# Sums of weight blocks in two seven-product SwiGLUs: VectorE additions replaced by accumulating transfers

## The chip, the cores and the metric

One core of one Trainium2 chip runs the whole program in one launch. The metric is the device time of that launch in microseconds (us). PE is TensorE's matmul side, PEld its weight loading, DVE is VectorE, ACT is ScalarE, POOL is GpSimd, SP is SyncE, whose queue issues all the transfers of the kernel before.

## The reference

The program computes two layers of a hybrid backbone over 512 latent tokens and 256 context tokens of width 1024, in float32. Each layer is a half-step SwiGLU, a token-mixing block (Fourier mixing, latent attention, windowed attention) and a second half-step SwiGLU. What matters here is the SwiGLU:

```
def swiglu(x, w1, w3, w2):
    return (jax.nn.silu(x @ w1) * (x @ w3)) @ w2

def macaron_half(h, m, i, g, w1, w3, w2):
    y = swiglu(modulate(rms_norm(h, g), m[:, 3 * i], m[:, 3 * i + 1]), w1, w3, w2)
    return h + 0.5 * m[:, 3 * i + 2, None, :] * y
```

The hidden width is 2816, that is 22 blocks of 128 columns of w1 and w3. The last SwiGLU of the program needs the 512 latent tokens alone; the first SwiGLU of the second layer works on all 768 tokens.

## The kernel before, in words

All activations are kept transposed, 128 features by tokens. Each float32 operand of a matmul is split into a high and a low part (float32r), and three matmuls (high by high, high by low, low by high) stand for one exact product: `mm3`, lines 396 to 398. A weight block of 128x1024 is loaded by SP into a buffer called `raw` (five buffers, `raws=5`, line 314) and split into a buffer called `w` (four buffers, `wslots=4`): the high part by an ACT cast (line 403, or line 406 with a scale), the low part by a DVE subtraction (line 404, or 407). After the subtraction the raw buffer is free; after the last matmul that reads it, the w buffer is free.

Two of the four SwiGLUs, both in the second layer, are written with seven block products in place of eight (`ffn7`, line 806): the first over all 768 tokens (halves of 384 columns), the second over the 512 latent tokens (halves of 256 columns). In them the 22 blocks of hidden columns are taken as 11 pairs. The first pair is plain (`first_pair`). Each of the other ten (`pair`, line 950) has four weight blocks a11, a12, a21 and a22 of 128x1024, and seven products, each of 24 matmuls, in this order of the program: B11 with a11, B21 with a12, E with minus (a21 + a22 + a11), t3 with (a11 + a21), t1 with (a21 + a22), t4 with a22, B22 with (a21 + a22 + a11 + a12). The products go to two PSUM tiles X and Y. Several of them add on top of what is there after ScalarE has copied the old content out (`snapshot`, line 876): E and t1 add to Y, t4 adds to X, so t4 has to wait for the copy of X that is made after t3. `gated` adds, applies silu and multiplies (lines 883 to 885); `parts` splits the result (lines 857, 858).

Between B11 and B21 in program order stands `middle()`: the down projection of the pair before, with two more weight blocks of w2 through the same raw and w buffers (`unit`, line 384) and 8 outputs per stream, each of six matmuls into one of four PSUM banks B and one DVE evacuation (line 895). So a pair takes weights in this order: a11, two blocks of w2, a12, then what E, t3, t1, t4 and B22 need.

The order of instructions on each engine is set by a scheduler that goes by priority (program order) and by its own estimate of when operands are ready; on the chip each engine runs its queue strictly in that order. Which buffer of `raw` or `w` a tile gets is whichever comes free, in that same order.

In the kernel before, the sums are made by four DVE additions per pair (lines 967, 968, 969 and 971) in a fifth raw tile `s1` and, in place, in the loaded blocks.

Of the kernel before, what the change touches and what calls it, by code (L numbers as in the profile page):

```python
# [12 lines left out]
ALU = mybir.AluOpType  # L13
# [299 lines left out]
class Builder:  # L313
# [480 lines left out]
    def block(self, src):  # L794

        r = self.mp.tile([128, 1024], F32, tag="raw", name=self.name("raw"), bufs=self.raws)
        if src is not None:
            self.nc.sync.dma_start(r, src)
        return r

    def split_block(self, r, scale=None):
# [4 lines left out]
    def ffn7(self, l, i, n, t, gate, nxt, streams=(X_COLS, C_COLS), split=None, late=None):  # L806
# [10 lines left out]
        nc = self.nc  # L817
        mp13, w2 = self.a["w13s"][i], self.a["w2"][l, i]
# [26 lines left out]
        def operand(name, k):  # L845
            tile_, cols = {"B11": (n[k], n1), "B21": (n[k + 4], n1), "B22": (n[k + 4], n2),
                           "t1": (tt.get((k, "u")), n1), "t3": (tt.get((k, "u")), n2),
                           "t4": (tt.get((k, "v")), n1), "E": (tt.get((k, "v")), n2)}[name]
            return [p[:, cols] for p in tile_]


        def gtiles(j):
            for f in (2 * j, 2 * j + 1):
                g[f] = self.hl(T, "g")

        def parts(f, s, cols):
            nc.scalar.copy(g[f][0][:, cols], s[:, cols])  # L857
            nc.vector.tensor_sub(g[f][1][:, cols], s[:, cols], g[f][0][:, cols].bitcast(F32))

        def product(bank, w, name, start):  # L860

            for x in range(2):
                for k in range(4):
                    self.mm3(bank[:, x * 512:x * 512 + wd], [w[:, p, x * 512 + k * 128:x * 512 + k * 128 + 128] for p in range(2)],
                             operand(name, k), start and k == 0, k == 3, not start)
# [7 lines left out]
        def snapshot(bank, base):  # L873
            y = self.m3(2 * wd, base=base)
            v = y.rearrange("p (x c) -> p x c", x=2)
            nc.scalar.copy(v, both(bank))
            return y, v

        def gated(s, cols, bank, y, sign):

            z = self.m3(2 * wd, base="z")
            zv = z.rearrange("p (x c) -> p x c", x=2)
            nc.vector.tensor_tensor(out=zv, in0=both(bank), in1=y[1], op=ALU.add)
            self.last_silu = nc.scalar.activation(s[:, cols], zv[:, 0], AF.Silu, scale=sign)
            nc.vector.scalar_tensor_tensor(out=s[:, cols], in0=zv[:, 1], scalar=sign, in1=s[:, cols], op0=ALU.mult, op1=ALU.mult)
            self.free(z)
# [59 lines left out]
        def done_with(j, name):  # L946
            if j == np_ - 1:
                self.free([tt.pop((k, name)) for k in range(4)])

        def pair(j, middle):  # L950
            fs = (2 * j, 2 * j + 1)
            src = mp13[j]
            add = nc.vector.tensor_add
            Y, X = (self.ps("S", (j + x) % 2) for x in range(2))
            r11 = self.block(src[0, 0])
            product(Y, self.split_block(r11), "B11", True)
            middle()
            y0 = snapshot(Y, "y")
            gtiles(j)
            s = [self.m3(base="silu") for _ in range(2)]  # L960
            r12 = self.block(src[0, 1])
            product(X, self.split_block(r12), "B21", True)
            r21, r22, s1 = self.block(src[1, 0]), self.block(src[1, 1]), self.block(None)
            gated(s[0], n1, X, y0, 1.0)
            self.free(y0[0])
            parts(fs[0], s[0], n1)
            add(s1, r21, r22)
            add(r21, r11, r21)
            add(r11, s1, r11)
            product(Y, self.split_block(r11, -1.0), "E", False)  # L970
            add(r12, r11, r12)
            y1 = snapshot(Y, "y")
            product(X, self.split_block(r21), "t3", True)
            w0 = snapshot(X, "y")
            product(Y, self.split_block(s1), "t1", False)
            done_with(j, "u")
            gated(s[1], n2, Y, w0, -1.0)
            self.free(w0[0])
            product(X, self.split_block(r22), "t4", False)
            done_with(j, "v")  # L980
            gated(s[1], n1, X, y1, -1.0)
            self.free(y1[0])
            parts(fs[1], s[1], slice(halves[0][0], halves[1][1]))
            product(Y, self.split_block(r12), "B22", False)
            self.last_silu = nc.scalar.activation(s[0][:, n2], Y[:, 0:wd], AF.Silu)
            nc.vector.tensor_mul(s[0][:, n2], s[0][:, n2], Y[:, 512:512 + wd])
            parts(fs[0], s[0], n2)
            self.free(s)
# [6 lines left out]
        def middle(j):  # L995
            def go():
                ws, fs = second(j), (2 * j, 2 * j + 1)
                for d in range(8):
                    for cols in streams:
                        down(fs, ws, d, cols)  # L1000
                self.free([g.pop(f) for f in fs])
            return go

        for j in range(1, np_ - 1):
            pair(j, middle(j - 1))

        fs = (NF - 2, NF - 1)
        if x_only:
            pair(np_ - 1, middle(np_ - 2))
        else:  # L1010
            held = {}

            def go():
                held["ws"], held["fs"] = second(np_ - 2), (NF - 4, NF - 3)
                for d in range(8):
                    down(held["fs"], held["ws"], d, X_COLS)

            pair(np_ - 1, go)
            for d in range(8):
                down(held["fs"], held["ws"], d, C_COLS)  # L1020
            self.free([g.pop(f) for f in held["fs"]])
# [878 lines left out]
```

## Time and profile before

| | us |
|---|---|
| median of 3 runs | 2759.79 |
| lowest and highest run | 2757.23 to 2761.97 |
| the profiled execution, its own time | 2759.59 |
| its span, first to last instruction | 2757.9 |

In the profiled execution TensorE's matmuls are busy for 2681.3 us (97% of the span), VectorE 1937.3 us (70%), ScalarE 1015.0 us (37%) and GpSimd 280.6 us (10%). The mean granted TensorE clock was 0.988. All transfers but the instruction fetches are issued by SP. A busy share is an average over stages with different limits; a stage is read from the stretch in which it runs. The pairs of the first seven-product SwiGLU lie between about 1610 and 2060 us, those of the second between about 2433 and 2730 us.

### The profile page before, as it was taken

Reading aid. Unit: us, or ns where it says so; the run is one execution under the profiler, and the core shown is the slowest. Engines: PE = TensorE matmul, PEld = TensorE weight load, DVE = VectorE, ACT = ScalarE, POOL = GpSimd, SP = SyncE. Lnnn points to the kernel's source line nnn. Section 1 sums busy time; section 2 is a strip of 40 time slices with the busy share of each in tenths; the row PEclk is TensorE's granted clock in tenths of the full one; section 3 lists DMA queues with packets and bytes.
Section 4 is the critical chain, followed back from the end, with each engine's and each line's share of the span. In section 5 each row is a group of like instructions: output and inputs, shape, how many; then the busy total and the mean of one; then the engine's idle time right before and its main releaser. Section 6 shows DMA issues by size and latency. Waiting matters only on the chain.

```text
span 2757.9 us, 40164 instructions
## 1 busy us (share of the span) xinstructions
PE 2681.3 (97%) x16028; PEld 2346.5 (85%) x16028; DVE 1937.3 (70%) x3385; ACT 1015.0 (37%) x1773; POOL 280.6 (10%) x372
## 2 busy tenths in 40 slices
PE   7999999999989999999999999999999989999999
PEld 5788888888867788888888889999998777889998
DVE  8986776655685658988663687676756675598886
ACT  4411211124665642111121443333335665554443
POOL 5100000011352210000000100000001352100000
PEclk9899999999989999999999999999999999999999
DMA  7432433211200025545321111212122210123322
GB/s 247 163 131 99 152 124 102 90 54 60 73 24 23 13 88 181 168 136 198 125 92 62 54 54 62 76 61 72 62 76 67 70 32 24 39 71 114 99 93 91
DMA packets 78671, 249.60 MB, mean 91 GB/s; under 512 B 8978, under 2 KB 10642, under 8 KB 78484
## 3 DMA queue, kind: packets, MB, share of 16 engines
q1 hardware_dynamic: 78484, 247.03, 27.1%
q8 instruction: 126, 2.06, 0.3%
q14 instruction: 61, 0.50, 0.1%
HBM read 244.90 MB, written 2.10 MB: 90 GB/s over the span
## 4 chain that ended last, share of the span: by engine, by line
PE 88%; DVE 6%; ACT 2%; issue 2%; DMA 1%; POOL 1%; SPq 0%; DVEq 0%; ACTq 0%; POOLq 0%
PE S L398 16%; PE S L396 16%; PE S L397 16%; PE B L396 11%; PE B L398 11%; PE B L397 11%; PE B L1409 3%; PE B L1560 2%; DVE w L404 1%; PE B L1528 1%; DVE junk L483 1%; ACT P L1397 0%; PE B L1453 0%; ACT w L403 0%; DMA ada<-in_w_ada 0%
## 5 line engine op out<-in xcount | busy, mean ns | idle before, releaser
L403 ACT CAST w<-raw 128x1024 fp32r<-128x1024 f32 x349 | 359.6, 1043 | 961.6 <-issue 539.0
L397 PE MATMUL S<-nlo,w 128*128 128x256 f32 (+2 forms) x1968 | 653.9, 333 | 7.0 <-DVE nlo L605 4.0
L398 PE MATMUL S<-nhi,w 128*128 128x256 f32 (+2 forms) x1968 | 652.5, 332 | 1.8 <-DVE w L404 1.7
L396 PE MATMUL S<-nhi,w 128*128 128x256 f32 (+2 forms) x1968 | 644.3, 333 | 9.1 <-DVE silu L915 3.9
L404 DVE TENSOR_TENSOR w<-raw,w 128x1024 fp32r<-128x1024 f32 x349 | 424.0, 1227 | 119.3 <-ACT w L403 117.1
L398 PE MATMUL B<-ghi,w 128*128 128x512 f32 (+1 forms) x1232 | 425.1, 346 | 0.8 <-DVE w L404 0.8
L397 PE MATMUL B<-glo,w 128*128 128x512 f32 (+1 forms) x1232 | 425.8, 346 | 0.0
L396 PE MATMUL B<-ghi,w 128*128 128x512 f32 (+1 forms) x1232 | 419.9, 348 | 2.7 <-ACT ghi L857 2.0
L397 PEld LDWEIGHTS S<-nlo,w 128*128 128x128 f32 x1968 | 371.9, 189 | 44.3 <-DVE nlo L605 7.5
L396 PEld LDWEIGHTS S<-nhi,w 128*128 128x128 f32 x1968 | 369.1, 189 | 45.0 <-DVE silu L915 4.5
L398 PEld LDWEIGHTS S<-nhi,w 128*128 128x128 f32 x1968 | 372.0, 189 | 38.8 <-DVE w L404 6.4
L691 DVE SCALAR_TENSOR_TENSOR h<-B,g,h 128x512 f32<-128x512 f32 (+1 forms) x352 | 208.2, 615 | 179.2 <-PE B L398 178.7
L396 PEld LDWEIGHTS B<-ghi,w 128*128 128x128 f32 x1232 | 230.6, 188 | 33.5 <-ACT ghi L857 2.4
L398 PEld LDWEIGHTS B<-ghi,w 128*128 128x128 f32 x1232 | 231.9, 188 | 31.2 <-DVE w L404 1.0
L397 PEld LDWEIGHTS B<-glo,w 128*128 128x128 f32 x1232 | 232.0, 188 | 30.2 <-issue 1.0
L895 DVE SCALAR_TENSOR_TENSOR h<-B,g,h 128x512 f32<-128x512 f32 (+1 forms) x264 | 170.1, 658 | 121.4 <-PE B L398 121.1
L483 DVE CUSTOM_DVE_ANT_0 junk<-ada,bc,mpart 128x768 f32<-128x768 f32 x238 | 245.6, 1032 | 6.3 <-DMA ada<-in_w_ada 1.3
L532 POOL TENSOR_TENSOR sq<-sq,sq 128x512 f32<-128x512 f32 (+1 forms) x38 | 42.8, 1126 | 1134.8 <-ACT sq L528 1133.7
L483 DVE CUSTOM_DVE_ANT_0 junk<-ada,bc,sml 128x256 f32<-128x256 f32 x238 | 118.7, 499 | 19.9 <-DMA ada<-in_w_ada 15.0
L1392 DVE TENSOR_REDUCE nm<-S 128x1 f32<-128x768 f32 (+3 forms) x120 | 94.5, 793 | 42.0 <-PE S L398 33.0
L1403 POOL TENSOR_SCALAR P<-P,rd 128x768 f32<-128x768 f32 (+3 forms) x120 | 96.7, 808 | 240.0 <-DVE rd L1402 185.1
L1397 ACT ACTIVATE P<-S,nm 128x768 f32<-128x768 f32 (+3 forms) x120 | 93.0, 776 | 56.0 <-DVE nm L1392 31.6
(273 smaller groups left out, 4450.2 us busy)
## 6 DMA issues: line engine op xcount, KB each, us to landing
raw<-in_w SPq DMA_DIRECT2D x176, 512.0 KB, 3.6
ada<-in_w_ada SPq DMA_DIRECT2D x171, 384.0 KB, 4.3
raw<-in_w13s SPq DMA_DIRECT2D x88, 512.0 KB, 3.7
raw<-in_w_out SPq DMA_DIRECT2D x16, 512.0 KB, 4.1
ada<-in_ada SPq DMA_DIRECT2D x16, 384.0 KB, 6.6
raw<-in_w_in_t SPq DMA_DIRECT2D x10, 512.0 KB, 3.5
raw<-in_dftx SPq DMA_DIRECT2D x8, 512.0 KB, 3.5
ada<-in_ada SPq DMA_DIRECT2D x8, 256.0 KB, 5.6
```

What stands on the lines that cost most here:

```text
L396: mm(out, lhs[0], rhs[0], start=start, stop=False, skip_group_check=more)
L397: mm(out, lhs[0], rhs[1], start=False, stop=False, skip_group_check=more)
L398: mm(out, lhs[1], rhs[0], start=False, stop=stop, skip_group_check=more)
L403: nc.scalar.copy(hi, src)
L404: nc.vector.tensor_sub(lo, src, hi.bitcast(F32))
L483: nc.vector.tensor_tensor_reduce(out=self.junk[:, 0:w.shape[1]], in0=w, in1=v, scale=1.0, scalar=init, op0=ALU.mult, op1=ALU.add, accum_ou ...
L691: nc.vector.scalar_tensor_tensor(out=self.h[d][:, c0:c1], in0=ps[:, 0:c1 - c0], scalar=gate()[:, d, s:s + 1], in1=self.h[d][:, c0:c1], op0 ...
L895: nc.vector.scalar_tensor_tensor(out=self.h[d][:, c0:c1], in0=ps[:, 0:c1 - c0], scalar=gate()[:, d, s:s + 1], in1=self.h[d][:, c0:c1], op0 ...
L1392: self.last_max = nc.vector.tensor_reduce(out=nm, in_=ps[:, c0:c1], axis=AX.X, op=ALU.max, negate=True)
L1397: self.last_exp = nc.scalar.activation(P, ps[:, c0:c1], AF.Exp, bias=nm, scale=1.0, accum_out=den)
L1403: nc.gpsimd.tensor_scalar(out=P, in0=P, scalar1=rd, scalar2=1.0, op0=ALU.mult, op1=ALU.mult)
L1409: mm(outs[y], lhs[y], rhs[y], start=start, stop=stop)
```

## The change

The four DVE additions go. A new helper, `block_sum`, loads the first block of a sum with a plain transfer from SP and then adds each further block with a transfer issued from GpSimd's queue that accumulates into the same raw buffer. Blocks that are in several sums are loaded again for each. Everything else (splits, products, copies, gating) stays.

```
     def block(self, src):
         r = self.mp.tile([128, 1024], F32, tag="raw", ...)
-        if src is not None:
-            self.nc.sync.dma_start(r, src)
+        self.nc.sync.dma_start(r, src)
+        return r
+
+    def block_sum(self, *srcs):
+        r = self.block(srcs[0])
+        for src in srcs[1:]:
+            self.nc.gpsimd.dma_start(out=r, in_=src, accum_op=ALU.add)
         return r
...
-            src = mp13[j]
-            add = nc.vector.tensor_add
+            (a11, a12), (a21, a22) = ([mp13[j, m, q] for q in range(2)] for m in range(2))
...
-            r11 = self.block(src[0, 0])
-            product(Y, self.split_block(r11), "B11", True)
+            product(Y, self.split_block(self.block(a11)), "B11", True)
...
-            r12 = self.block(src[0, 1])
-            product(X, self.split_block(r12), "B21", True)
-            r21, r22, s1 = self.block(src[1, 0]), self.block(src[1, 1]), self.block(None)
+            product(X, self.split_block(self.block(a12)), "B21", True)
...
-            add(s1, r21, r22)
-            add(r21, r11, r21)
-            add(r11, s1, r11)
-            product(Y, self.split_block(r11, -1.0), "E", False)
-            add(r12, r11, r12)
+            product(Y, self.split_block(self.block_sum(a21, a22, a11), -1.0), "E", False)
             y1 = snapshot(Y, "y")
-            product(X, self.split_block(r21), "t3", True)
+            product(X, self.split_block(self.block_sum(a11, a21)), "t3", True)
             w0 = snapshot(X, "y")
-            product(Y, self.split_block(s1), "t1", False)
+            product(Y, self.split_block(self.block_sum(a21, a22)), "t1", False)
...
-            product(X, self.split_block(r22), "t4", False)
+            product(X, self.split_block(self.block(a22)), "t4", False)
...
-            product(Y, self.split_block(r12), "B22", False)
+            product(Y, self.split_block(self.block_sum(a21, a22, a11, a12)), "B22", False)
```

## Rows read from the trace of the kernel before

**Rows 1.** The profile's page: the span, and TensorE's part of its first section.

```profile
span 2757.9 us, 40164 instructions
...
PE 2681.3 (97%) x16028; PEld 2346.5 (85%) x16028; DVE 1937.3 (70%) x3385; ACT 1015.0 (37%) x1773; POOL 280.6 (10%) x372
```

**Rows 2.** Busy time by stretch: stretch, length, engines, granted clock, DMA share, GB/s.

```profile
1610.00:2060.00 450.00, 448.60 (x2546) 427.26 (x2545) 304.61 (x385) 144.96 (x185) 0.00 (x0) 1.00 0.21 68
2464.00:2712.00 248.00, 247.66 (x1712) 228.27 (x1711) 200.55 (x245) 104.74 (x151) 0.00 (x0) 1.00 0.32 103
2433.00:2464.00 31.00, 29.73 (x206) 27.12 (x205) 28.42 (x36) 13.87 (x20) 0.00 (x0) 1.00 0.31 102
```

**Rows 3.** DVE groups by line, 2464 to 2712 us: count, busy, mean ns, idle before.

```profile
L404 DVE TENSOR_TENSOR w<-raw,w 128x1024 fp32r<-128x1024 f32 x63 | 75.5, 1220 | 10.5 <-ACT w L403 10.5
...
L971 DVE TENSOR_TENSOR raw<-raw,raw 128x1024 f32<-128x1024 f32 x8 | 9.8, 1226 | 0.3
L967 DVE TENSOR_TENSOR raw<-raw,raw 128x1024 f32<-128x1024 f32 x8 | 9.8, 1226 | 2.4 <-DMA raw<-in_w13s 1.7 <-DVE silu L885 0.6
L968 DVE TENSOR_TENSOR raw<-raw,raw 128x1024 f32<-128x1024 f32 x8 | 9.7, 1219 | 0.0
L969 DVE TENSOR_TENSOR raw<-raw,raw 128x1024 f32<-128x1024 f32 x8 | 9.7, 1216 | 0.0
```

**Rows 4.** Line 798, the loads of the blocks a11 to a22, whole span.

```profile
L798 SPq DMA_DIRECT2D raw<-in_w13s x88: 327/328/328, 1499.6 to 2706.4; - x88
...
DMA to landing us min/median/max: 3.3/3.7/5.5
```

**Rows 5.** SP's queue in order of time, 2430 to 2560 us: one pair to the next.

```profile
2500.98 11.13 SPq L388 DMA_DIRECT2D raw<-in_w  x2
2512.92 18.12 SPq L798 DMA_DIRECT2D raw<-in_w13s  x4
2532.51 11.15 SPq L388 DMA_DIRECT2D raw<-in_w  x2
```

**Rows 6.** ScalarE in order of time, one pair of the second SwiGLU.

```profile
2540.73 2.00 ACT L403 CAST w<-raw 128x1024 fp32r<-128x1024 f32 x2 [7.47 <-PE B L398]
2542.63 0.58 ACT L876 COPY y<-S 128x512 f32<-128x512 f32 x1
2543.11 1.05 ACT L403 CAST w<-raw 128x1024 fp32r<-128x1024 f32 x1
2544.50 0.59 ACT L876 COPY y<-S 128x512 f32<-128x512 f32 x1 [0.34 <-PE S L398]
...
2553.33 1.04 ACT L403 CAST w<-raw 128x1024 fp32r<-128x1024 f32 x1
...
2559.15 1.06 ACT L406 ACTIVATE w<-raw 128x1024 fp32r<-128x1024 f32 x1 [2.67 <-DVE raw L969]
```

**Rows 7.** VectorE in order of time, the same pairs.

```profile
2529.47 1.21 DVE L407 SCALAR_TENSOR_TENSOR w<-raw,w 128x1024 fp32r<-128x1024 f32 x1
2530.61 0.74 DVE L895 SCALAR_TENSOR_TENSOR h<-B,g,h 128x512 f32<-128x512 f32 x1
...
2542.09 3.49 DVE L404 TENSOR_TENSOR w<-raw,w 128x1024 fp32r<-128x1024 f32 x3
...
2555.77 1.22 DVE L404 TENSOR_TENSOR w<-raw,w 128x1024 fp32r<-128x1024 f32 x1
```

**Rows 8.** TensorE in order of time: first down matmul, first of t4, first of B22.

```profile
2528.38 0.39 PE L397 MATMUL B<-glo,w 128*128 128x512 f32 x1
...
2547.14 0.28 PE L396 MATMUL S<-cvhi,w 128*128 128x256 f32 x1
...
2550.00 0.28 PE L396 MATMUL S<-nhi,w 128*128 128x256 f32 x1
```

**Rows 9.** Busy time by stretch: the program's first loads, all engines of DMA at work.

```profile
14.00:18.00 4.00, 2.93 (x14) 2.84 (x15) 3.58 (x8) 3.17 (x5) 0.00 (x0) 1.00 1.02 400
```

**Rows 10.** GpSimd's groups by line, whole span: its longest and its shortest instructions.

```profile
L475 POOL TENSOR_TENSOR mprod<-ada,bc 128x768 f32<-128x768 f32 x14 | 30.7, 2203 | 32.0 <-DMA ada<-in_ada 20.2 <-issue 8.5 <-DVE a L236 2.6
...
L1403 POOL TENSOR_SCALAR P<-P,rd 128x256 f32<-128x256 f32 x24 | 11.4, 478 | 23.5 <-DVE rd L1402 14.8 <-PE B L1495 2.5 <-ACT es L1400 1.8
```

**Rows 11.** ScalarE in order of time, one pair of the first SwiGLU.

```profile
1703.97 1.04 ACT L403 CAST w<-raw 128x1024 fp32r<-128x1024 f32 x1
...
1733.33 2.00 ACT L403 CAST w<-raw 128x1024 fp32r<-128x1024 f32 x2
```

## The prediction

> **What bounds the kernel now.** I read the page's first section first: matmuls are busy for 97% of the span [rows 1], so only a stage in which TensorE waits can gain much. Then the stretches of the two edited SwiGLUs [rows 2]. In the first, TensorE is busy 448.6 of 450 us; in the second 247.7 of 248 us over about eight pairs, after a first pair with 29.7 of 31. The granted clock is 1.00 throughout, its upper level of 2.4 GHz. VectorE is busy for two thirds to four fifths there, and GpSimd runs nothing. The reader should see that VectorE is not the bound of these pairs: its four additions [rows 3] have almost no idle time ahead of them and none of it reaches TensorE. What could be won in these stretches is TensorE's whole idle time, 1.4 + 0.3 + 1.3 = 3.0 us.
>
> Next I read how far ahead of TensorE the weights are. The queue of SP [rows 5] shows a pair of the second SwiGLU every 31.5 us (2500.98 to 2532.51). Six loads per pair, 512 KB each, keep the DMA engines busy for 0.32 of the time [rows 2]. A load lands 3.7 us after its issue, 3.3 at best and 5.5 at worst [rows 4]. The kernel is bound by TensorE with weights that are ready early, and the question is whether they still are.
>
> **Removed.** Four additions of 1.22 us [rows 3] in each of 20 pairs: 20 x 4 x 1.22 = 98 us of VectorE time. TensorE's work hides it, so it is worth at most the 3.0 us above; I take 1.5.
>
> **Added.** Per pair the loads of a11 to a22 go from 4 plain ones to 7 plain ones from SP and 7 accumulating ones from GpSimd; with the two blocks of w2 that is 16 transfers in place of 6. Three more issues on SP, 0.33 us each [rows 4], delay nothing, because that queue spends its time waiting for buffers. Five raw buffers now serve 9 tiles per pair; before it was 7. GpSimd's queue is empty in these stretches [rows 2], so nothing else waits behind the new instructions. But an accumulation cannot start before the one ahead of it in the same buffer has landed. So GpSimd's queue waits, and the sums behind the waiting one (t3 and t1 behind E, then B22) wait with it. B22 is a chain of one load and three accumulations.
>
> **Price of one accumulation, x.** The trace has no transfer from GpSimd and none that adds, so I bound it. It moves the same bytes as a load, which takes 3.7 us [rows 4]; I see no reason for less. Above that come two unknowns. It may also have to read the destination: 0 to one more pass of the engines, where a pass is 0.32 x 248 / 48 loads = 1.65 us [rows 2]. And GpSimd has to prepare it: from nothing to its longest instruction, 2.2 us; its short ones take 0.48 us [rows 10]. So x lies between 3.7 and 3.7 + 1.65 + 2.2 = 7.5 us. I take a full second pass and a preparation near the short instructions: 3.7 + 1.65 + 0.65 = 6.0 us.
>
> The Trainium skill, page "DMA: Bandwidth & Descriptors", section "Anatomy of one DMA — SWDGE (gpsimd) path", gives 2.0 us plus the bytes over 436 GB/s for one transfer from GpSimd, which is an estimate of 3.2 us for these blocks, without the addition. By it the chain of B22 would be hidden and the time unchanged; no run here shows it yet, and the sum does not use it.
>
> **Does it fit?** In the second SwiGLU, B22's raw buffer is the one that a12 gives back. (Five tiles earlier: a12, E, t3, t1, t4, B22.) a12 is cast at 2553.33 [rows 6], and its subtraction ends at 2555.77 + 1.22 = 2557.0 [rows 7]. The cast of B22 stands at 2543.11 in the pair before [rows 6], so at 2574.6 in this one. Between them lie 17.6 us; a load and three accumulations need 3.7 + 3x. Up to x = 4.6 us nothing waits. Beyond it ScalarE stands at B22's cast, and behind that cast in its queue is the copy of X (2544.50), which t4 needs at 2547.14 [rows 6, 8]. The copy is done 0.6 us after its start, so the cast may begin 2.4 us late: up to x = 5.4 us this is hidden as well. Beyond that, t4 and everything after it on TensorE is late. The late end also delays a12's split of the next pair, so it is a loop: each pair takes 31.5 + 3 (x - 5.4) us.
>
> A second wait runs into the same one. E's buffer comes from the B22 before it, free at 2542.09 + 3.49 = 2545.6 [rows 7]; its load and two accumulations are ready at 2549.3 + 2x, and its cast is at 2559.15 [rows 6], so x = 4.9 us is where VectorE begins to stand at E's subtraction. Behind that is the first evacuation of the down projection, 1.1 us later [rows 7]. Four banks cover it for a few us, and a pair that is stretched by the first loop gives this one the same time back, so I add nothing for it.
>
> In the first SwiGLU the same loop has more room: from a12's split (cast at 1703.97, done some 3 us later) to B22's cast (the second of two from 1733.33, so 1734.3) are 27.4 us [rows 11], which fit up to x = 7.9 us. I count nothing there.
>
> **Sum.** 3 x (6.0 - 5.4) = 1.8 us per pair, ten pairs: +18. Less 1.5 for the additions: 2759.59 + 16.5 = 2776 us against the profiled execution, whose time stands 0.2 us from the median of the runs.
>
> **Rivals.**
>
> *Hidden after all (not slower).* If x is at most 5.4 us, nothing reaches TensorE, and the 3.0 us of idle time bound the gain: 2757 to 2762 us. For it: an unloaded transfer lands in 3.3 us, and the preparation may overlap the wait. The same comes out at x = 6.0 if the scheduler puts B22's cast behind the copy of X. Then only the product's own start counts, 2550.00 + 31.5 [rows 8] less 2.3 us for cast and subtraction, which fits up to x = 6.2 us. Against it: 16 transfers per pair share the engines, and B22's first accumulation queues behind those of t3 and t1.
>
> *The DMA engines become the bound.* If an accumulation reads source and destination one after the other, it costs two passes. By the share of the rows nine plain transfers take 9 x 1.65 = 14.9 us and seven doubled ones 23.1 us: 38.0 us in a pair of 31.5 us, 6.5 us x 10 pairs = +65, 2825 us. Against it: with many loads at once the engines moved 400 GB/s [rows 9], 1.31 us per block, by which it is 9 x 1.31 + 7 x 2.62 = 30.1 us and still fits, barely. It decides from some 2.4 to 2.8 us of engine time per accumulation. The Trainium skill, "Collectives: The Full Stack", section "The bandwidth ceiling", says that a reducing transfer needs two source reads on the same ring and so runs at half the rate of a copy; that speaks for this rival, and no row of this trace bears on it.
>
> *A slow accumulation.* At the upper end, x = 7.5 us, the loop gives 3 x 2.1 x 10 = +63, 2822 us, with the first SwiGLU still just clear of it.
>
> *Faster.* More than 0.2% would need 5.5 us, and both stretches hold 3.0 us of idle time; only another order of instructions elsewhere could give the rest.
>
> **How the numbers follow.** About 0.2% (5.5 us) is what a measurement of this kernel can tell from no change. Chances: an accumulation of 5.5 to 6.8 us, slower by up to 42 us, 0.41; hidden, 0.38; engines bound or x above 6.8 us, 0.18; faster 0.03. Of the first case a little (0.01) lies under 5.5 us. So faster 0.03, same 0.39, slower 0.58. I predict the likeliest case, 2776 us, its own range 2762 to 2801. The range over the cases goes from 2756 (the hidden case with nearly the whole 3.0 us gained) to 2825 (the engines bound by the rows' share, and the upper bound of x).
>
> **What would show it.** Right: DVE lines 967 to 971 gone; GpSimd with 140 transfers; in the second SwiGLU pairs of about 33 us, ScalarE idle ahead of B22's cast with an accumulating transfer as releaser, TensorE idle ahead of t4; the first SwiGLU with pairs as before. Hidden: pairs of 31.5 us and accumulations that land in 5 us. Engines bound: a DMA share near 1 in the second SwiGLU, plain loads that land in much more than 3.7 us, waits spread over all weights. Wrong altogether: waits in the first SwiGLU too, so x above 7.9 us, or an order in GpSimd's queue that holds one sum behind another.

## The result, and the profile after

The changed kernel takes 2840.31 us (median of 4 runs, 2829.44 to 2846.82) against 2759.67 us before: a ratio of 1.0284, 95% interval 1.0264 to 1.0305. The forecast was 2776 us in 2756 to 2825; the direction and the place were right, the size was not, and the time lies 15 us beyond the range.

First the profile's page of the changed kernel: the span and engine totals, beside [rows 1], then GpSimd's DMA queue (packets, MB, the share of 16 engines' span), and two issue rows with the median us from issue to landing.

```profile
span 2836.2 us, 40637 instructions
...
PE 2707.3 (95%) x16028; PEld 2365.6 (83%) x16028; DVE 1852.5 (65%) x3305; ACT 1016.6 (36%) x1773; POOL 403.6 (14%) x512
...
q0 software_dynamic: 20160, 73.41, 14.9%
...
raw<-in_w13s SPq DMA_DIRECT2D x148, 512.0 KB, 4.9
raw<-in_w13s POOLq DMA_DIRECT2D x140, 512.0 KB, 6.7
```

VectorE's busy time is 85 us lower, and that bought nothing: the span is 78 us longer, while TensorE's busy time grew by 26 us.

Busy time by stretch, in the columns of [rows 2]: the first seven-product SwiGLU, then the second.

```profile
1610.00:2060.00 450.00, 449.28 (x2553) 428.45 (x2554) 264.50 (x343) 143.43 (x185) 58.75 (x67) 1.00 0.76 180
2482.00:2770.00 288.00, 248.18 (x1564) 224.73 (x1563) 150.16 (x198) 96.97 (x137) 43.90 (x51) 0.92 0.85 210
```

The first is as before: TensorE busy for all but 0.7 us. The second was busy for 247.7 of 248 us; now 40 of 288 us are idle, and the granted clock is 0.92. SP's queue gives the pair there, beside [rows 5]:

```profile
2482.25 6.02 SPq L388 DMA_DIRECT2D raw<-in_w  x2
...
2761.72 6.50 SPq L388 DMA_DIRECT2D raw<-in_w  x2
```

From the first of these rows to the second are seven pairs: 279.47 / 7 = 39.9 us each, in place of 31.5. Ten pairs 8.4 us longer would be 84 us, close to the loss of 80.6 us.

What sets the 39.9 us is in the chain of work that ended last (start, us, what):

```profile
2547.53 1.05 ACT w L403
2548.60 1.24 DVE w L404
2549.85 8.00 DMA raw<-in_w13s
2557.92 0.60 issue
2558.52 5.47 DMA raw<-in_w13s
2563.99 0.39 issue
2564.38 5.49 DMA raw<-in_w13s
2569.88 0.39 issue
2570.27 7.36 DMA raw<-in_w13s
2577.87 0.78 issue
2578.66 0.59 ACT y L882
2579.29 0.39 PE S L396
...
2587.90 9.05 DMA raw<-in_w13s
```

Read it as a ring: a12 is cast and subtracted, its buffer takes B22's load, three accumulations follow one at a time, then come the copy of X, t4 and B22 (2579.29 to 2585.27), and the next a12 is cast and subtracted. This turn of the ring takes 38.05 us (2549.85 to 2587.90), and its chain 27.8 us (2549.85 to 2577.63), of which the load alone takes 8.00. Each accumulation follows the transfer before it after 0.4 to 0.7 us, so GpSimd's queue did not hold this chain back. The turn before took longer, 46.0 us (2503.89 to 2549.85), with a chain of 33.7 us:

```profile
2503.89 8.60 DMA raw<-in_w13s
...
2528.66 8.89 DMA raw<-in_w13s
```

Six of B22's chains lie on the chain of work that ended last; their loads took 8.0 to 9.05 us. In three of the pairs after 2617 us it runs through E's sum and its cast instead, as here:

```profile
2636.61 1.06 ACT w L406
```

ScalarE's queue at the end of B22's chain, beside [rows 6]:

```profile
2577.70 1.04 ACT L403 CAST w<-raw 128x1024 fp32r<-128x1024 f32 x1 [5.93 <-DMA raw<-in_w13s]
2578.66 0.58 ACT L882 COPY y<-S 128x512 f32<-128x512 f32 x1
```

ScalarE stood 5.93 us at B22's cast, and the copy of X follows right behind it, as the prediction had them. TensorE's waits in 2482 to 2770 us (who waited for what: total us, times, longest) show that most of its idle time is not ahead of t4 (line 882) but ahead of E's product, for E's cast and subtraction (lines 406, 407):

```profile
PE S L396 <- ACT w L406: 25.0, 7, 4.9
PE S L396 <- ACT y L882: 10.2, 5, 5.0
PE S L398 <- DVE w L407: 4.4, 7, 0.8
```

How long a load or an accumulation takes depends on what runs beside it. GpSimd's queue in one early pair of the first SwiGLU:

```profile
1666.38 0.88 POOL L804 DMA_DIRECT2D raw<-in_w13s  x1 [10.12 <-DVE h L901]
1672.15 0.87 POOL L804 DMA_DIRECT2D raw<-in_w13s  x1 [4.89 <-DMA raw<-in_w13s]
```

There, with no other transfer issued beside them, one accumulation follows another after 5.77 us. In the second SwiGLU one lands 5.2 us after its issue at best, 7.1 in the median, 9.7 at worst, and a plain load of the same blocks takes 5.2 us in the median where it took 3.7 [rows 4]. These medians mix several chains. B22's load is among the slowest of the plain ones: it is issued while the sums of E, t3 and t1 are under way, and in its 8 us the DMA share (second number from the end) is 1.04, all the engines at work:

```profile
2549.85:2557.85 8.00, 8.00 (x47) 6.96 (x46) 0.92 (x2) 0.59 (x1) 1.77 (x2) 1.00 1.04 254
```

### The profile page after: what moved, and what is told of

Its sections match the earlier page's. It is cut to its first block, busy times and chain, and to the rows that moved or that the text cites. A ratio compares the mean times of both kernels' runs of the same rounds, so it can differ in the third digit from the quotient of the medians.

```text
span 2836.2 us, 40637 instructions
## 1 busy us (share of the span) xinstructions
PE 2707.3 (95%) x16028; PEld 2365.6 (83%) x16028; DVE 1852.5 (65%) x3305; ACT 1016.6 (36%) x1773; POOL 403.6 (14%) x512
## 3 DMA queue, kind: packets, MB, share of 16 engines
q0 software_dynamic: 20160, 73.41, 14.9%
## 4 chain that ended last, share of the span: by engine, by line
PE 77%; DMA 9%; DVE 7%; ACT 3%; issue 3%; POOL 1%; SPq 0%; ACTq 0%; POOLq 0%; DVEq 0%
PE S L396 14%; PE S L398 14%; PE S L397 14%; PE B L396 10%; PE B L397 10%; PE B L398 10%; DMA raw<-in_w13s 8%; PE B L1407 3%; PE B L1558 2%; DVE w L404 1%; PE B L1526 1%; ACT w L403 1%; DVE junk L483 1%; DVE nm L1390 0%; ACT P L1395 0%
## 5 line engine op out<-in xcount | busy, mean ns | idle before, releaser
L397 PE MATMUL B<-glo,w 128*128 128x512 f32 (+1 forms) x1232 | 432.6, 351 | 0.0
L398 PE MATMUL B<-ghi,w 128*128 128x512 f32 (+1 forms) x1232 | 431.3, 351 | 0.8 <-DVE w L404 0.8
L396 PE MATMUL B<-ghi,w 128*128 128x512 f32 (+1 forms) x1232 | 426.6, 354 | 3.4 <-ACT ghi L863 2.9
L396 PEld LDWEIGHTS B<-ghi,w 128*128 128x128 f32 x1232 | 234.7, 192 | 36.2 <-ACT ghi L863 3.3
L398 PEld LDWEIGHTS B<-ghi,w 128*128 128x128 f32 x1232 | 236.1, 192 | 33.1 <-DVE w L404 1.0
L804 POOL DMA_DIRECT2D raw<-in_w13s x140 | 122.7, 914 | 779.7 <-DMA raw<-in_w13s 525.3
L396 PE MATMUL S<-cvhi,w 128*128 128x384 f32 (+1 forms) x320 | 104.4, 326 | 48.9 <-ACT w L406 31.6
```

The source lines that it names most:

```text
L396: mm(out, lhs[0], rhs[0], start=start, stop=False, skip_group_check=more)
L397: mm(out, lhs[0], rhs[1], start=False, stop=False, skip_group_check=more)
L398: mm(out, lhs[1], rhs[0], start=False, stop=stop, skip_group_check=more)
L804: self.nc.gpsimd.dma_start(out=r, in_=src, accum_op=ALU.add)
```

## The experiments

Theory 1 is the prediction's ring: the chain of B22 through a12's buffer, ending in ScalarE's queue. Theory 2: the DMA engines' load sets the pair. Theory 3: being issued from GpSimd costs the time, not adding. Theory 4: E's late sum sets it. In the diffs "-" is the changed kernel unless another is named. Plain_gpsimd, no_t3_t1_sums, b22_one_less and e_one_less leave terms out of the sums, as their diffs show; the others compute the whole reference.

**plain_gpsimd.** The same 140 transfers, without the addition.

```
-            self.nc.gpsimd.dma_start(out=r, in_=src, accum_op=ALU.add)
+            self.nc.gpsimd.dma_start(out=r, in_=src)
```

> GpSimd's transfers overwrite instead of adding, so the sums are left out (each buffer ends with its last block); queue, count and order of waits stay. If the addition in the transfer is the cost (both theories: a second pass of the engines), a transfer from GpSimd lands in some 4.5 to 5 us in place of 6.7 and the time goes to 2760 to 2775 us. Theory 3 (the software path): preparation by GpSimd and its queue are the cost, landing stays above 6 us and the time above 2800 us.

2768.84 us, ratio 1.0027 (1.0012 to 1.0043). Its page and its chain of work, one B22 chain:

```profile
q0 software_dynamic: 20160, 73.41, 7.7%
```

```profile
2530.50 5.61 DMA raw<-in_w13s
2536.17 0.61 issue
2536.79 4.37 DMA raw<-in_w13s
2541.15 0.39 issue
2541.55 4.48 DMA raw<-in_w13s
2546.02 0.39 issue
2546.42 4.48 DMA raw<-in_w13s
```

Some 71 of the 80 us belong to the addition, so theory 3 falls. The shares price it: 14.9% of 2836.2 us over 140 transfers is 3.02 us of all 16 engines for an accumulation, 7.7% of 2770.3 us is 1.52 us for the same bytes unadded. And the ring's formula can be tried: this chain lasts 20.4 us (2530.50 to 2550.90). The prediction gave the chain 17.6 + 2.4 = 20.0 us before a pair grows, so 31.5 + 0.4 = 31.9 us; SP's rows show 32.2.

**first_only.** Accumulating in the first SwiGLU, VectorE's four additions in the second.

```
+            if not x_only:
                 ... block_sum(...) as changed
+            else:
+                ... the four additions of the kernel before
```

> The first seven-product SwiGLU accumulates in transfers, the second has VectorE's additions as before. Every theory here puts the whole loss into the second SwiGLU, whose pairs last 31.5 us against 46 in the first: 2756 to 2763 us, no difference from the kernel before. If part of the loss is elsewhere (a first use of GpSimd's transfers, the mixing in between), it shows as the rest above that.

2760.78 us, ratio 1.0002 (0.9992 to 1.0011). The whole loss is the second SwiGLU's, and taking the additions off VectorE in the first (its busy time falls from 1937.3 to 1900.0 us) is worth nothing that can be measured.

**no_t3_t1_sums.** Two of seven additions per pair fewer, neither in B22's chain.

```
-  ... self.block_sum(a11, a21) ... "t3"    ... self.block_sum(a21, a22) ... "t1"
+  ... self.block(a11) ... "t3"             ... self.block(a21) ... "t1"
```

> t3 takes a11 alone and t1 takes a21 alone, so two of the seven additions are left out; B22's chain keeps its load and three accumulations. Theory 1 without contention (the chain's own latency): B22's chain shortens little, pairs of 36 us or more, 2800 us or more. Theory 1 with contention (the chain is long because t3's and t1's accumulations run beside it): its load falls from 8 to 5 us or less, pairs of 33 to 34 us, 2775 to 2790 us. Theory 2: engine time 9 x 1.55 + 5 x 3.0 = 29 us is below 31.5, so 2760 to 2770 us.

2820.19 us, ratio 1.0219 (1.0199 to 1.024). By the two shares, nine plain transfers and five accumulations are 9 x 1.52 + 5 x 3.02 = 28.8 us of engine time, under the old 31.5, and yet a pair takes 37.6 us. The engines' load alone does not set it. It does work on the chain: accumulations now land in 6.6 us in the median instead of 7.1, and the B22 loads issued at 2542.58 and 2581.34 us take 6.13 and 6.76 us instead of 8.0 to 9.05.

**b22_one_less and e_one_less.** One addition taken out of B22's chain, or out of E's.

```
-  self.block_sum(a21, a22, a11, a12)   (B22)
+  self.block_sum(a21, a22, a12)        (b22_one_less)
-  self.block_sum(a21, a22, a11)        (E)
+  self.block_sum(a21, a11)             (e_one_less)
```

> B22's sum leaves out a11: load and two accumulations instead of three, both SwiGLUs. Theory 1 (the loop through a12's buffer and B22's chain sets the pair): each of some nine pairs of the second SwiGLU is shorter by one accumulation, 5.5 to 6.5 us: 2780 to 2795 us. Theory 4 (E's late sum is the wait that counts, it is the larger one in the list of TensorE's waits): E's own chain stays as it is, 2820 us or more.

> E's sum leaves out a22: load and one accumulation instead of two. Theory 1: E's chain is not in the loop, so only the engines' load falls a little: 2825 to 2842 us. Theory 4: each pair is shorter by one accumulation: 2780 to 2795 us.

2811.79 us, 1.0185 (1.0165 to 1.0205), and 2851.46 us, 1.0327 (1.0303 to 1.0352). Both drop one addition, and so the same load; only the one in B22's chain gains, 28 us. In the other, TensorE's waits for E are gone and those of t4 for the copy of X have taken their place (10.2 us became 47.9), on the same ring; its 11 us more were not explained.

```profile
PE S L396 <- ACT y L882: 47.9, 7, 11.3
```

That speaks for theory 1 and against 2 and 4. But a whole x per pair was not gained, and the time lies between what the two theories had expected: pairs fall to 36.7 us, and TensorE then waits for E's cast (18.0 us in eight waits, 2482 to 2770 us). E's chain is the next limit, close behind.

**early_b22.** B22's load and accumulations begun ahead of E's.

```
+            r_b22 = self.block_sum(a21, a22, a11, a12)
             product(Y, self.split_block(self.block_sum(a21, a22, a11), -1.0), "E", False)
 ...
-            product(Y, self.split_block(self.block_sum(a21, a22, a11, a12)), "B22", False)
+            product(Y, self.split_block(r_b22), "B22", False)
```

> The sum of four blocks for B22 is begun before that of E in program order, so it takes a raw buffer some 14 us earlier; the same 16 transfers per pair. Theory 1 (the chain): the pair of the second SwiGLU lasts as long as B22's load and three accumulations behind a12's buffer; with the earlier buffer that chain is hidden and only E's remains: 2765 to 2790 us. Theory 2 (the engines): a pair of transfers costs 9 x 1.55 + 7 x 3.0 = 35 us of engine time in whatever order, so no pair can take less: 2795 us at the best, rather 2840 as before.

2921.33 us, ratio 1.058 (1.0555 to 1.0606): the total missed what both theories expected. In the second SwiGLU the pairs did fall, to 36.5 us; but the first broke. Its stretch, and TensorE's longest wait there:

```profile
1610.00:2060.00 450.00, 386.00 (x2113) 363.35 (x2113) 219.62 (x290) 121.82 (x155) 48.24 (x55) 0.92 0.60 149
```

```profile
PE B L396 <- DVE h L901: 62.6, 7, 9.8
```

E's sum, now begun later, holds ScalarE's cast (line 406) for 91.7 us in seven waits; the subtraction behind it holds VectorE, and behind that stand the evacuations of the down projection (line 901). That is the "second wait" to which the prediction added nothing. In the first SwiGLU of the changed kernel it was free only by its place in the order.

**b22_vector.** B22's sum by one VectorE addition, a12 + E's sum.

```
+            r_e = self.block_sum(a21, a22, a11)
+            product(Y, self.split_block(r_e, -1.0), "E", False)
+            nc.vector.tensor_add(r12, r12, r_e)
 ...
+            product(Y, self.split_block(r12), "B22", False)
```

> B22's sum is one VectorE addition of E's finished buffer to a12's, everything else accumulates in transfers; a pair has 12 transfers, four of them accumulating. Theory 1: the loop is gone, 2757 to 2770 us. Theory 4: E's chain is as long as before, 2800 us or more.

2792.46 us, ratio 1.0116 (1.0099 to 1.0133); it missed what was expected. The three accumulations of B22 are gone, and with them 48 of the 80 us; pairs take 34.5 us. What is left is E's chain: all of TensorE's longer waits are now for E's cast and subtraction (8.6 and 6.4 us).

**b22_own_buffer and b22_pinned.** B22's sum in two half-block buffers of its own, second SwiGLU only: allocated anew in each pair, or kept through the whole SwiGLU with the load at the start of the pair.

```
+            own = [self.m3(512, base="own") for _ in range(2)]     (in each pair, or once)
+            for x, r in enumerate(own):
+                nc.sync.dma_start(r, a21[:, x * 512:x * 512 + 512])
+            for src in (a22, a11, a12):
+                for x, r in enumerate(own):
+                    nc.gpsimd.dma_start(out=r, in_=src[:, ...], accum_op=ALU.add)
```

> In the second SwiGLU alone B22's sum gets a buffer of its own outside the five (two halves of 512 columns, so its transfers and its split come as halves) and is begun before E's sum; number of bytes and additions as in the changed kernel. Theory 1: with a buffer that is not given back by a12 the chain starts early and is hidden: 2762 to 2785 us. If the length of the chains or the engines' load as such were the bound, 2820 us or more.

> As the run with B22's own buffer, but that buffer (two halves of 512 columns) is kept for B22 alone through the whole second SwiGLU, so it is free again as soon as B22 of the pair before has been split, some 11 us earlier than a12's buffer; bytes and additions as in the changed kernel. Theory 1 (the moment at which the chain's buffer is given back, plus the chain, sets the pair): a chain of 22 to 28 us fits a pair of 31.5 us, nearly, and what stays is E's later sum, 2765 to 2800 us. If it is the chains' length or the engines' load as such, whatever the moment of the start: 2835 us or more.

2912.34 us, 1.0552 (1.0536 to 1.0568), and 2805.21 us, 1.0162 (1.0148 to 1.0176). The first missed: its buffers came free only at the end of the down projection, so the chain began later than a12's buffer would have let it, and pairs took 46.7 us. The second begins early: ScalarE's wait for B22's sum is all but gone (3.2 us in seven waits), pairs take 36.5 us, and E's wait is the longest left; the time is 5 us above what was expected. Here the load of the engines shows: the DMA share is 0.96.

```profile
2482.00:2770.00 288.00, 263.20 (x1720) 239.04 (x1720) 167.66 (x224) 105.19 (x160) 70.20 (x80) 0.96 0.96 233
```

So theory 2 is a floor behind the ring: 0.96 x 36.5 = 35.0 us of engine time per pair, and 9 x 1.52 + 7 x 3.02 = 34.8 by the shares. By this estimate no order of the instructions could bring back 31.5 us with seven accumulations in a pair.

**two_term_sums and two_term_early.** Only t3's and t1's sums accumulate, one addition each; E and B22 by two VectorE additions. In the second kernel s1 is begun ahead of a12's block.

```
+            s1 = self.block_sum(a21, a22)      (early: ahead of a12's block)
+            nc.vector.tensor_add(r11, r11, s1)
+            product(Y, self.split_block(r11, -1.0), "E", False)
+            nc.vector.tensor_add(r12, r11, r12)
 ...
+            product(Y, self.split_block(r12), "B22", False)
```

> Only the two sums of two blocks, for t3 and t1, accumulate in transfers, one accumulation each; E and B22 are made by two VectorE additions from them. Theory 1: no chain is longer than a load and one accumulation, some 11 us, so nothing reaches TensorE: 2757 to 2766 us, the kernel before within 0.2%. If an accumulating transfer costs TensorE something by itself, whatever its chain: two of seven are left, 2780 us or so.

> As the kernel with two sums of two terms in transfers and E and B22 by two VectorE additions, but the load and the accumulation of a21 + a22 stand ahead of a12's block in the program. Theory 1 (the sum lands after the place in VectorE's fixed order at which it is needed): the sum takes the buffer that is free before a12's, so the addition for E finds it landed; the second SwiGLU's pairs return towards 31.5 us, 2757 to 2775 us. Rival: if the buffer for it comes no earlier, or the wait moves to a12's load (whose buffer is then the later one) the pairs stay above 35 us and the time stays at 2800 us or more.

2818.01 us, 1.0207 (1.0191 to 1.0224), and 2795.98 us, 1.0136 (1.0121 to 1.015). The first missed: there is no long chain, the DMA share is 0.49, and still a pair takes 37.6 us. VectorE in order of time:

```profile
2540.86 1.22 DVE L972 TENSOR_TENSOR raw<-raw,raw 128x1024 f32<-128x1024 f32 x1 [6.27 <-DMA raw<-in_w13s]
...
2543.47 0.42 DVE L989 TENSOR_TENSOR silu<-silu,S 128x256 f32<-128x256 f32 x1
```

One addition has taken the place of B22's cast: it stands at the head of VectorE's queue until the accumulation lands, and behind it stands the gating (lines 891, 989) on which TensorE waits, 32.9 us in the stretch. The early start halves that wait (row below, two_term_early), and pairs take 34.3 us: a good third of the loss gone, but the sum is late still, and the expected 2757 to 2775 was missed by 21 us. Part of what is left is lost in the first SwiGLU, where TensorE is now busy for 441.2 of 450 us.

```profile
2576.87 1.23 DVE L972 TENSOR_TENSOR raw<-raw,raw 128x1024 f32<-128x1024 f32 x1 [3.42 <-DMA raw<-in_w13s]
```

**late_cast.** B22's split issued behind the copy of X, second SwiGLU only.

```
+            r_b22 = self.block_sum(a21, a22, a11, a12)
+            with self.tc.issue_after(x_copied.ins):      (if x_only)
+                w_b22 = self.split_block(r_b22)
-            product(Y, self.split_block(self.block_sum(a21, a22, a11, a12)), "B22", False)
+            product(Y, w_b22, "B22", False)
```

> In the second SwiGLU alone, ScalarE's cast of the four-term sum for B22 is issued behind the copy of X; all transfers stay. Theory 1 (the loop runs from the landing of B22's sum through ScalarE's queue to t4): t4 no longer waits for the sum. From the landing to the start of B22's product there were the cast 1.04, the copy 0.6 and t4's 24 matmuls 2.9 us; now only the cast and a subtraction, 2.3 us. So some 2.2 us less per pair: 37.7 us, 2815 to 2825 us, and the waits of TensorE ahead of t4 go to nearly nothing while waits for B22's own low part appear. Rival (theory 2, the transfers' rate alone sets the pair): pairs stay at 40 us and the time at 2835 to 2845 us.

2863.37 us, ratio 1.0377 (1.0363 to 1.0392): slower by 23 us, where either theory expected less or no change. T4's wait is gone as intended, but the same lateness comes out elsewhere. ScalarE's row and TensorE's waits:

```profile
2582.72 2.94 ACT L403 CAST w<-raw 128x1024 fp32r<-128x1024 f32 x3 [10.08 <-DMA raw<-in_w13s]
```

```profile
PE S L396 <- DVE z L889: 55.0, 7, 9.2
```

ScalarE now stands 10 us at B22's cast, with two other casts behind it; VectorE stands 11 us at their subtractions, and behind these is the reading of PSUM (line 889) that TensorE needs before it may go on. The queues' order is fixed when the program is made; to move the consumer of a late sum moves the wait and what it blocks.

## Why the prediction was wrong in size

**TensorE bound, VectorE's additions hidden: right.** 85 us of VectorE time went, and nothing was gained in the first SwiGLU (449.28 of 450 us) or in first_only.

**The ring in the second SwiGLU: right, with its formula.** The forecast was 31.5 us plus what the chain takes beyond 20.0 us. In plain_gpsimd a chain of 20.4 us gives 31.9 against 32.2 measured. In the changed kernel 27.8 us give 39.3 against 38.05 for that turn of the ring, and 33.7 us give 45.2 against 46.0 for the turn before. The copy of X behind B22's cast, and t4 behind the copy, are in the rows as named.

**The step that failed: the price of the chain, above all of its load.** The chain was put at a plain load of 3.7 us and three accumulations of x = 6.0 us, 21.7 us, with little beside them. In the chain shown the load took 8.00 us, and the accumulations 19.8 us with the issues between them (2557.85 to 2577.63), 6.6 us each: 27.8 us. Of the 6.1 us more, the load has 4.3 and the accumulations 1.8. That makes +78 us over ten pairs in place of +18. In the six chains named above the load takes 8.0 to 9.05 us and x is 6.3 to 8.4 us, in five of them under the upper end given, 7.5. So x was put a little low, and the load at less than half of what it became. Where nothing else is issued beside them, in the first SwiGLU at 1666 us, the accumulations need 5.77 us each, near 6.0.

The cause is the change itself: 16 transfers per pair, seven of them at twice the engine time, raise the DMA share from 0.32 [rows 2] to 0.85, and to 1.04 while B22's load is on its way. Two accumulations fewer shortened that load (no_t3_t1_sums). The prediction counted the sharing as an argument for the slow rivals and left the likeliest case at the unloaded prices; the rival with x = 7.5 kept the load at 3.7 us too, so the range stopped at 2825.

**The first SwiGLU free up to x = 7.9: right** (pairs as before, TensorE busy throughout), though by little: a chain there takes 25.8 us (1657.39 to 1683.15) of the 27.4 us given.

**E's wait adds nothing: right for the sum, wrong as a margin.** One term less in E gains nothing. But the banks did not cover it: TensorE idles 29.4 us ahead of E's product in seven pairs, and only 10.2 us ahead of t4, where the prediction had put its wait. E's chain becomes the limit as soon as B22's is shorter, at some 34 to 37 us per pair (b22_vector, b22_one_less, b22_pinned), and it is what broke early_b22.

**The rivals.** Hidden: no, except without the addition. Engines bound: not what set the time, but real as a floor of 34.8 us per pair; the prediction's two estimates for it, 38.0 and 30.1, stand on either side. The Trainium skill, "Collectives: The Full Stack", section "The bandwidth ceiling", has the reduce step of a collective at half the rate of its copy step, because it needs two source reads. The shares of the accumulating transfers here agree, 3.02 against 1.52 us; why they take twice the time was not tested. The Trainium skill's price in "DMA: Bandwidth & Descriptors", section "Anatomy of one DMA — SWDGE (gpsimd) path", an estimate of 3.2 us per block, lies below what plain_gpsimd shows in the chain (4.4 to 4.5 us).

**The clock.** TensorE's granted clock fell behind some of these waits, which the prediction did not count. Three stretches of the changed kernel, the first two with about t4's 24 matmuls in each, the third behind E's cast and subtraction:

```profile
2539.20:2543.90 4.70, 4.68 (x22) 4.68 (x23) 4.03 (x5) 2.28 (x3) 0.00 (x0) 0.50 0.53 140
2579.30:2582.20 2.90, 2.90 (x24) 2.90 (x25) 2.69 (x4) 1.96 (x3) 0.00 (x0) 1.00 0.36 90
2561.30:2563.90 2.60, 2.60 (x8) 2.21 (x9) 2.60 (x5) 0.00 (x0) 0.00 (x0) 0.50 0.97 238
```

The first ran at 0.50, the lower level of 1.2 GHz, after a wait of 5.0 us; the second, after a wait of 2.5 us, at 1.00; the third, after waits of 1.5 and 0.8 us, at 0.50 again. So the length of the last wait alone does not tell the level. At the lower level t4 took 2 us longer. By count, TensorE's busy time per pair rose from 31.5 to 248.18 / 288 x 39.9 = 34.4 us, 2.9 of the 8.4 us; how much of that lies on the ring was not taken apart.

**Left open.** How much of the longer landing is queueing in the 16 engines and how much sharing of their rate was not separated. The changed kernel with B22's load alone made earlier or faster was not run, so the split of the loss between load and accumulations is read from the traces. More raw buffers in place of borrowed ones were not tried.

## What to carry to other kernels

A sum moved from an engine into accumulating transfers turns work that overlaps into a chain that does not: each term waits for the one before to land. Price that chain with the landing times of the traffic that the change itself creates, ask from which moment its buffer is free, and look up what stands behind its consumer in that engine's fixed queue. When one engine has time to spare, as VectorE had here, leave the sums with it: none of the kernels that accumulated in the second SwiGLU came back to the time before.

## What the runs showed of the hardware

An accumulating transfer of 128x1024 float32 from GpSimd's queue occupies the 16 engines for 3.02 us, twice the 1.52 us of the plain one; its issue holds GpSimd for 0.87 us instead of 0.53. With nothing else issued beside them, chained ones follow every 5.77 us; at a DMA share of 0.85 they land in 7.1 us in the median, and plain loads beside them in 5.2 instead of 3.7 us. A plain load issued while the share stood at 1.04 took 8.0 us. In the three granted-clock rows above, matmuls ran at half the clock after a wait of 5.0 us and after waits of 1.5 and 0.8 us, and at the full clock after one of 2.5 us.
